# Stores of the pair matrices from another queue, other costs in the scheduler, and weight loads with a lead

## Chip, cores and metric

The kernel runs on one core of a Trainium2 chip. The time is that of one execution on the device, in microseconds. TensorE (PE) multiplies matrices, ScalarE (ACT) and VectorE (DVE) work on vectors, GpSimd (POOL) has little to do here, and SyncE (SP) issues transfers (DMAs).

## What is computed

Two layers of a network run over 1024 latent tokens and 256 context tokens of 1024 channels. One projection of the normalised input feeds four groups; group A is a gated DeltaNet over chunks of 64 tokens, in both directions, and it is the one that the change touches:

```python
decay = jnp.exp(jnp.where(incl, gcum[..., :, None] - gcum[..., None, :], -jnp.inf))
lmat = -jnp.where(strict, jnp.einsum('bnhid,bnhjd->bnhij', kb, kc) * decay, 0.0)
for _ in range(GDN_CHUNK_LOG2 - 1):      # tinv = (1 - lmat)^-1
    power = power @ power
    tinv = tinv + tinv @ power
attn = jnp.einsum('bnhid,bnhjd->bnhij', qc, kc) * decay
```

`lmat` and `attn` are the pair matrices, one of 64 x 64 for each chunk, head and direction. Groups B, C and D are convolutions and a gated MLP. All groups are gated by SiLU, joined, and go through one output projection, whose result is added to the input.

## The kernel before

In layer 0 the DeltaNet of the context stream (4 chunks) runs first and then that of the latent stream (16 chunks); so in layer 1. The dense projections of the other groups, 24 matmuls of 128 x 512 for a block (three for each of 8 slices of the weights, which are held as a high and a low part), are what PE does beside them.

A helper records every operation (so nearly all of them have line 215 in the profile), and a list scheduler, `schedule`, then puts them in one order for each engine. It goes by the costs of `estimate`, by a fixed price for a DMA, and by a priority: the place in the program plus a `boost`, a lower number going first. Where an operation can run on ACT or on DVE, it picks one. Each engine takes its instructions in that order. A DMA signals on one of eight semaphores, taken in turn in program order, and waits for the DMA eight before it, whichever queue that one is on.

The DeltaNet of a latent stream goes through these steps:

- `pair_matrices` runs eight times, for two chunks in each direction. It takes four of the six buffers `b` of 128 x 512: `gx` and `rw` are products made on DVE, PE sums `gx` up, ACT takes the exponential, DVE multiplies it in, PE multiplies keys and queries, and DVE masks the product and transposes it. Then it issues eleven stores on SP: two of `rw` into `at` (128 x 256, 128 KB each), and for each of three matrices into `zd` one of 128x2x64 (64 KB) and two of 64x2x64 (32 KB). The buffers come free when the stores have landed. Over both layers and streams these are 216 stores.
- `invert` runs twice (calls 1 to 4 of `pair_matrices` into the first half, 5 to 8 into the second). It loads blocks of 32 x 32 from `zd` into `u` (four loads), inverts them on DVE in 30 steps of two operations, and stores the result in `zb`.
- `scan` prepares each group of chunks: it loads from `zb`, transposes on DVE, and multiplies on PE (`ax<-b,b`, the first such matmul is where the preparation begins), and then goes through the chunks.

In the trace's names, in the latent stream of layer 0, the two halves of `zd` are `zd_550` and `zd_576`, the blocks are in `u_549`, the first inverse goes to `zb_580`, and `b_596` and `b_609` are temporaries of the two inversions.

Weights come in by `pump`: it loads them into one of two buffers `r` (512 KB), and `split` makes the high part on ACT (a cast, `w<-r`) and the low part on DVE. Only the split has a boost, of -600 (`AHEAD_SPLIT`).

Of the kernel before, what the change touches and what calls it, by code (L numbers as in the profile page):

```python
# [41 lines left out]
TC, G = 64, 4  # L42
# [37 lines left out]
class Program:  # L80
# [60 lines left out]
    def estimate(self, eng, method, out, ins, args, kw):  # L141
# [4 lines left out]
        if eng == "PE":  # L146
            if method == "transpose":
                return 0.12
            lhsT, rhs = ins[0], ins[1]
            n, m, k = self.cols(rhs), self.cols(lhsT), lhsT.shape[0]  # L150
            if "r" in str(rhs.dtype).split("float32")[-1]:
                return max(0.107, n / 2400.0 + 0.0133)
            if m <= 64 or k <= 64:
                return max(0.116, 0.01 + n * 4 / 2400.0) / (4 if self.quads else self.side_by_side(k, m))
            return max(0.214, n * 4 / 2400.0) if n > 16 else 0.4
        if eng == "ACT":
            return (0.051 if ps else 0.093) + n / 1200.0 + 0.093 * (ptr + acc)
        if eng == "DVE":
            if method == "reciprocal":
                return 0.07 + n * 0.00625  # L160
            if method in ("tensor_scalar", "tensor_copy") and not ps:
                return 0.069 + n / 1920.0 + 0.06 * ptr
            return 0.069 + n / 960.0 + 0.06 * ptr
# [23 lines left out]
    def add(self, calls):  # L187
# [16 lines left out]
        if eng == "SP":  # L204
            n = args[0].size() if callable(args[0].size) else args[0].size
            run = min(x.ap[-1][1] if x.ap[-1][0] == 1 else 1 for x in (args[0], args[1]))
            op.dma = n * 4 / 360e3 * (1.0 if run >= 128 else 2.0)
        for e, m, fn, ar, k in calls:
# [5 lines left out]
            cost = 0.475 if e == "SP" else self.estimate(e, m, o[0], n, ar, k)  # L214
# [43 lines left out]
    def schedule(self):  # L258
# [50 lines left out]
        while len(order) < len(ops):  # L309
# [68 lines left out]
            if e == "SP":  # L378
# [5 lines left out]
            for u in op.users:  # L384
                o = ops[u]
                o.ready_from.append((i, op.finish if e == "SP" else
# [80 lines left out]
class Block:  # L467
# [375 lines left out]
    def dense(self, items):  # L843
# [5 lines left out]
        def pump(i):  # L849
            while True:  # L850
# [13 lines left out]
                if q < min(i + 6, n) and self.room("r")() and (items[q].cond is None or items[q].cond()):  # L864
                    raws[q] = r = self.take("r", [P] + items[q].shape)
                    items[q].load(r)
                    st["l"] += 1
# [607 lines left out]
    def pair_matrices(self, st, c0, gi, s0, need_q):  # L1475
# [32 lines left out]
        if need_q:  # L1508
            nc.vector.tensor_tensor(rw, both(0), dm, ALU.mult)
            for d in range(2):  # L1510
                nc.sync.dma_start(st.at[d, :, c0:c0 + 2], rw[:, d].rearrange("p (c h) i -> p c (h i)", h=2))
        z = self.blk([P, 4, TC])
        nc.vector.transpose(z.rearrange("p a i -> p (a i)"), gx[:, 1].rearrange("p a i -> p (a i)"))
        for d, t in ((0, gx[:, 0]), (1, gx[:, 1]), (2, z)):
            to = zd[d, 2 * s0:2 * s0 + 4].rearrange("(c h) p i -> h p c i", h=2)
            t = t.rearrange("p (c h) i -> p h c i", h=2)
            nc.sync.dma_start(to[0], t[:, 0])
            for p in range(2):
                nc.sync.dma_start(to[1, (1 - p) * TC:(2 - p) * TC], t[p * TC:(p + 1) * TC, 1])
# [649 lines left out]
```

## Time and profile before

| what | value |
|---|---|
| median of 3 runs | 1415.69 us (1413.28 to 1418.06) |
| the profiled execution | 1418.21 us, of which the span 1416.1 |
| mean granted clock of PE | 0.943 |
| PE busy | 1277.3 us, 90% of the span |
| DVE busy | 986.6 us, 70% |
| ACT busy | 544.9 us, 38% |

Busy times are shares of the whole span. They say nothing of the stages, in which other engines wait or are waited for; the rows below are taken by stage. A row of the timeline has its start and its length, then engine, line and operation, `out<-in`, and how many instructions it joins; in brackets the idle time before it and what ended that. SPq is the time in which SP issues, no DMA's own duration.

### The profile page before, as it was taken

The page shows a single profiled execution, that of the slowest core. Times are in us where ns is not written, and L with a number is a line of the kernel's source. Part 1 is how long each engine was busy: PE and PEld are TensorE (multiplying, and loading weights), DVE is VectorE, ACT ScalarE, POOL GpSimd, SP SyncE. Part 2 cuts the span into 40 slices and gives each one's busy share as a digit, 9 for nine tenths or more (in the row PEclk, how much of TensorE's full clock was granted, in tenths as well). Part 3 has the DMA queues.
Part 4 walks back from the last instruction along what each step waited for, and adds up shares of the span by engine and source line. Part 5 has one row for each costly group of instructions (what it writes and reads, how often), then busy time and mean ns, then how long its engine had stood idle before and what let it go on. Part 6 is the DMA issues. An engine that isn't in the chain of part 4 may idle for free.

```text
span 1416.1 us, 27022 instructions
## 1 busy us (share of the span) xinstructions
PE 1277.3 (90%) x10888; PEld 1003.2 (71%) x10888; DVE 986.6 (70%) x2112; ACT 544.9 (38%) x917; POOL 11.9 (1%) x76
## 2 busy tenths in 40 slices
PE   6886699999988899999998999989998759999997
PEld 3875577986766655568886778978666646678886
DVE  4787969998855755573376669899776677784454
ACT  3876632254633122132154444343455303231221
POOL 1000000000000000000000000000000000000000
PEclk9997799999996889999999999999999779999999
DMA  9646332322447466573233332334226535132832
GB/s 310 182 108 183 108 89 62 88 46 58 104 105 172 121 178 193 179 223 104 90 112 109 114 104 63 67 81 101 62 50 147 136 85 127 51 105 89 262 84 56
DMA packets 310386, 166.75 MB, mean 118 GB/s; under 512 B 150174, under 2 KB 294902, under 8 KB 310262
## 3 DMA queue, kind: packets, MB, share of 16 engines
q1 hardware_dynamic: 310262, 165.03, 42.9%
q8 instruction: 85, 1.39, 0.4%
q14 instruction: 39, 0.32, 0.1%
HBM read 124.32 MB, written 35.42 MB: 113 GB/s over the span
## 4 chain that ended last, share of the span: by engine, by line
PE 52%; DVE 20%; DMA 12%; SPq 7%; ACT 5%; issue 4%; DVEq 0%; ACTq 0%; POOL 0%; POOLq 0%
PE mm L215 37%; DVE u L215 10%; PE sc L215 10%; SPq L215 7%; PE ax L215 5%; DVE b L215 5%; DMA x<-u 3%; DMA r<-in_w_in 3%; DVE w L215 2%; ACT b L215 1%; DMA u<-zd 1%; ACT L215 1%; DMA zd<-b 1%; ACT u L215 1%; DMA u<-in_x 1%
## 5 line engine op out<-in xcount | busy, mean ns | idle before, releaser
L215 PE MATMUL mm<-hh,w 128*128 128x512 f32 x1664 | 553.9, 407 | 6.8 <-ACT g L215 4.2
L215 PEld LDWEIGHTS mm<-hh,w 128*128 128x128 f32 x1664 | 316.1, 192 | 92.0 <-issue 20.8
L215 PE MATMUL mm<-hl,w 128*128 128x512 f32 x832 | 338.8, 407 | 1.5 <-issue 1.5
L215 PE MATMUL mm<-u,w 128*128 128x512 f32 (+1 forms) x1320 | 264.9, 359 | 13.9 <-ACT w L215 8.7
L215 PEld LDWEIGHTS mm<-u,w 128*128 128x128 f32 x1320 | 222.0, 195 | 48.1 <-ACT w L215 8.9
L215 DVE SCALAR_TENSOR_TENSOR u<-u,pv,u 128x1024 f32<-128x1024 f32 (+1 forms) x172 | 202.7, 1187 | 1.3 <-ACT u L215 0.6
L215 PEld LDWEIGHTS mm<-hl,w 128*128 128x128 f32 x832 | 159.9, 192 | 41.1 <-issue 9.4
L215 ACT CAST w<-r 128x1024 fp32r<-128x1024 f32 x88 | 92.5, 1052 | 249.5 <-PE mm L215 177.0
L215 DVE TENSOR_TENSOR w<-r,w 128x1024 fp32r<-128x1024 f32 x88 | 107.5, 1222 | 40.1 <-ACT w L215 39.8
L215 ACT ACT_TABLE_LOAD x87 | 111.6, 1283 | 21.4 <-DMA zd<-b 11.3
L215 DVE TENSOR_TENSOR u<-u,b 128x256 f32<-128x256 f32 (+26 forms) x246 | 90.1, 387 | 28.1 <-DMA u<-in_x 17.9
L215 ACT ACTIVATE b<-u 128x512 f32<-128x512 f32 (+1 forms) x71 | 42.5, 610 | 66.5 <-DVE u L215 45.5
L215 PE MATMUL mm<-u,u 128*128 128x256 f32 (+1 forms) x384 | 58.7, 303 | 5.7 <-ACT u L215 4.3
L215 DVE TENSOR_TENSOR b<-u 128x198 f32<-128x198 f32 (+24 forms) x180 | 56.9, 331 | 8.5 <-DMA u<-zd 6.9
L215 PEld LDWEIGHTS mm<-u,u 128*128 128x128 f32 x384 | 52.0, 201 | 9.0 <-ACT u L215 4.7
L215 PE MATMUL sc<-ident,b 128*128 128x128 f32 (+1 forms) x139 | 27.5, 322 | 25.2 <-ACT b L215 10.2
L215 PE MATMUL mm<-u,hh 128*128 128x272 f32 x256 | 48.5, 289 | 0.0
L215 PEld LDWEIGHTS sc<-v,u 64*64 64x64 f32 x1184 | 34.4, 140 | 19.6 <-DVE v L215 11.2
L215 PE MATMUL sc<-v,u 64*64 64x64 f32 x1184 | 42.9, 228 | 5.0 <-issue 4.0
L215 ACT COPY v<-sc 128x256 f32<-128x256 f32 x36 | 13.4, 372 | 78.6 <-PE sc L215 69.4
L215 ACT ACTIVATE b<-sc,mod,modG 128x128 f32<-128x128 f32 x86 | 35.0, 456 | 19.4 <-PE sc L215 11.0
L215 PEld LDWEIGHTS sc<-ident,b 128*128 128x128 f32 (+1 forms) x139 | 18.9, 163 | 32.6 <-ACT b L215 13.5
(273 smaller groups left out, 1455.6 us busy)
## 6 DMA issues: line engine op xcount, KB each, us to landing
r<-in_w_in SPq DMA_DIRECT2D x90, 512.0 KB
u<-in_w_ada SPq DMA_DIRECT2D x16, 1024.0 KB
u<-in_x SPq DMA_DIRECT2D x16, 512.0 KB
r<-ylat SPq DMA_DIRECT2D x16, 512.0 KB
ylat<-g SPq DMA_DIRECT2D x24, 256.0 KB
u<-in_w_out SPq DMA_DIRECT2D x12, 512.0 KB
at<-b SPq DMA_DIRECT2D x36, 128.0 KB
u<-at SPq DMA_DIRECT2D x18, 256.0 KB
```

Of the source, the lines that this page charges most:

```text
L215: op.alts[e] = ((lambda fn=fn, ar=ar, k=k: fn(*ar, **k)), cost, table)
```

## The change

The stores of `pair_matrices` are issued by `nc.scalar` in place of `nc.sync`, so that they stand in ACT's order. The costs in the scheduler are other numbers: a DMA's issue 0.62 in place of 0.475 us, on whichever engine, ACT's and DVE's fixed parts, small transposes on PE. The load of a weight in `pump` gets the same boost as its split.

```diff
             if method == "transpose":
-                return 0.12
+                return 0.11 if ins[0].shape[0] > 64 else 0.03
...
         if eng == "ACT":
-            return (0.051 if ps else 0.093) + n / 1200.0 + 0.093 * (ptr + acc)
+            return (0.155 if ps else 0.19) + n / 1200.0 + 0.05 * ptr + 0.093 * acc
         if eng == "DVE":
+            if n == 1:
+                return 0.155
...
+            if method == "tensor_tensor" and not ps and 128 < n <= 256:
+                return 0.4
...
-        if eng == "SP":
+        if method == "dma_start":
...
-            cost = 0.475 if e == "SP" else self.estimate(e, m, o[0], n, ar, k)
+            cost = 0.62 if method == "dma_start" else self.estimate(e, m, o[0], n, ar, k)
...
-            if e == "SP":
+            if op.dma:
                 dma_free = max(dma_free, t + 1.1) + op.dma
...
                     raws[q] = r = self.take("r", [P] + items[q].shape)
+                    self.nc.boost -= AHEAD_SPLIT
                     items[q].load(r)
+                    self.nc.boost += AHEAD_SPLIT
...
-                nc.sync.dma_start(st.at[d, :, c0:c0 + 2], rw[:, d].rearrange("p (c h) i -> p c (h i)", h=2))
+                nc.scalar.dma_start(st.at[d, :, c0:c0 + 2], rw[:, d].rearrange("p (c h) i -> p c (h i)", h=2))
...
-            nc.sync.dma_start(to[0], t[:, 0])
+            nc.scalar.dma_start(to[0], t[:, 0])
             for p in range(2):
-                nc.sync.dma_start(to[1, (1 - p) * TC:(2 - p) * TC], t[p * TC:(p + 1) * TC, 1])
+                nc.scalar.dma_start(to[1, (1 - p) * TC:(2 - p) * TC], t[p * TC:(p + 1) * TC, 1])
```

ACT in the latent stream of layer 0 before, from the exponential of the fifth call (`b_579`) to that of the sixth (`b_586`); `u_492` belongs to a convolution, `g_610` is a gate, `r` and `w` are weights:

```order
L215 ACTIVATE b_579<-ax_581 128x512
L215 ACT_TABLE_LOAD
L215 ACTIVATE u_492<-u_492 128x1024
L215 ACTIVATE g_610<-mm_608 128x512
L215 ACTIVATE g_610<-g_610,pv_71_166 128x512
L215 ACT_TABLE_LOAD
L215 ACTIVATE b_586<-sc_582 128x512
```

The same stretch of ACT now, from behind `b_579`, with the stores of the fifth call:

```order
L219 ACT_TABLE_LOAD
L219 ACTIVATE g_589<-mm_575 128x512
L219 ACTIVATE g_610<-mm_608 128x512
L219 DMA zd_576<-b_577 128x2x64
L219 DMA at_548<-b_578 128x256 x2
L219 DMA zd_576<-b_577 64x2x64 x2
L219 DMA zd_576<-b_577 128x2x64
L219 DMA zd_576<-b_577 64x2x64 x2
L219 DMA zd_576<-b_583 128x2x64
L219 DMA zd_576<-b_583 64x2x64 x2
L219 ACT_TABLE_LOAD
L219 ACTIVATE b_586<-sc_582 128x512
```

All eleven stores of a call now stand between its exponential and the next call's.

DVE in the same stream before, from the eighth call's mask and transpose (`b_599`, `b_603`) to the first steps of the first inversion (`b_596`); `x_637` and the rest belong to group D and the norms:

```order
L215 TENSOR_TENSOR b_599<-sc_602,b_601 128x512
L215 TENSOR_TENSOR b_600<-sc_602,b_601 128x512
L215 STREAM_TRANSPOSE b_603<-b_599 128x256
L215 TENSOR_TENSOR x_637<-sc_635,sg_411_508 128x256
L215 TENSOR_TENSOR x_637<-x_637,u_612 128x256
L215 TENSOR_SCALAR nq_517<-sc_617 128x16 x2
L215 TENSOR_TENSOR at_638<-sc_636,sg_411_508 128x256
L215 TENSOR_TENSOR b_596<-u_549 128x30
L215 TENSOR_TENSOR u_549<-u_549,b_596 128x30
L215 RECIPROCAL rn_421_518<-rn_421_518 128x32
L215 TENSOR_TENSOR b_596<-u_549 128x58
```

And now, around the same mask of the eighth call:

```order
L219 TENSOR_TENSOR u_549<-u_549,b_596 128x16x15
L219 TENSOR_TENSOR b_596<-u_549 128x240
L219 TENSOR_TENSOR u_549<-u_549,b_596 128x15x16
L219 TENSOR_TENSOR b_601<-b_601,b_600 128x512
L219 TENSOR_TENSOR b_596<-u_549 128x238
L219 TENSOR_TENSOR b_599<-sc_602,b_601 128x512
L219 TENSOR_TENSOR b_600<-sc_602,b_601 128x512
L219 STREAM_TRANSPOSE b_603<-b_599 128x256
L219 TENSOR_TENSOR w_658<-r_615,w_658 128x1024
L219 TENSOR_TENSOR x_637<-sc_635,sg_411_508 128x256
L219 TENSOR_TENSOR u_549<-u_549,b_596 128x14x17
L219 TENSOR_TENSOR x_637<-x_637,u_612 128x256
```

The eighth call's mask now stands between the two operations of the 17th of the first inversion's 30 steps, and the second inversion (`b_609`) begins when the first has ended, in place of running in turn with it.

SP ahead of the store of the first inverse, before:

```order
L215 DMA r_659<-in_w_in 128x8x128
L215 DMA gd_129<-g_657 64x512
L215 DMA r_702<-in_w_in 128x8x128
L215 DMA b_661<-in_smlp_w 128x4x128
L215 DMA zb_580<-u_549 128x1024
```

And now, with the block loads of the second inversion (`u_549<-zd_576`) ahead of it:

```order
L219 DMA gd_129<-g_645 64x512 x2
L219 DMA u_549<-zd_576 32x32x32 x3
L219 DMA b_628<-zd_550 32x8x32 x4
L219 DMA u_549<-zd_576 32x32x32
L219 DMA r_702<-in_w_in 128x8x128
L219 DMA gd_129<-g_657 64x512 x2
L219 DMA zb_580<-u_549 128x1024
```

The block loads wait for the stores of calls 5 to 8, and the store of the first inverse stands behind them.

On PE the first pair matmul of that stream moves from place 1881 to 1903 and the first matmul of the scan's preparation from 2386 to 2361. SP has 216 instructions less, ACT has 216 stores and 8 table loads more, and 52 operations move from ACT to DVE.

## Rows read from the trace of the kernel before

**Rows 1.** Windows: start:end, length; busy PE, PEld, DVE, ACT, POOL; PEclk; DMA; GB/s.
```profile
0.00:50.00 50.00, 34.33 (x262) 22.87 (x263) 24.46 (x100) 24.31 (x49) 3.75 (x36) 1.00 0.90 278
50.00:175.00 125.00, 89.94 (x683) 82.41 (x682) 105.35 (x296) 91.34 (x168) 1.34 (x6) 0.84 0.53 141
364.00:488.00 124.00, 108.27 (x699) 85.30 (x699) 86.98 (x203) 41.42 (x52) 0.31 (x2) 0.88 0.55 135
1044.00:1162.00 118.00, 91.36 (x597) 71.72 (x599) 86.52 (x193) 42.11 (x48) 1.47 (x7) 0.87 0.49 115
1275.00:1400.00 125.00, 125.00 (x553) 103.59 (x552) 60.33 (x112) 28.00 (x52) 0.00 (x0) 1.00 0.42 131
```

**Rows 2.** Timeline of PE: start, length; the scan's first preparation in either layer.
```profile
487.05 1.17 PE L215 MATMUL ax<-b,b 32*32 32x32 f32 x64 [3.25 <-DVE b L215]
1161.56 1.18 PE L215 MATMUL ax<-b,b 32*32 32x32 f32 x64 [12.20 <-DVE b L215]
```

**Rows 3.** Timeline of SP, first latent stream: first stores, last block loads, first inverse.
```profile
364.52 0.62 SPq L215 DMA_DIRECT2D zd<-b  x1
365.25 0.91 SPq L215 DMA_DIRECT2D at<-b  x2
...
421.82 5.11 SPq L215 DMA_DIRECT2D zd<-b  x8
...
436.31 2.03 SPq L215 DMA_DIRECT2D u<-zd  x3
...
475.42 0.46 SPq L215 DMA_DIRECT2D zb<-u  x1
```

**Rows 4.** Groups of ACT by form: count, busy us, mean ns, idle before them.
```profile
L215 ACT ACT_TABLE_LOAD x87 | 111.6, 1283 | 21.4 <-DMA zd<-b 11.3 <-DMA at<-b 3.5 <-DMA gd<-g 2.2
L215 ACT CAST w<-r 128x1024 fp32r<-128x1024 f32 x88 | 92.5, 1052 | 249.5 <-PE mm L215 177.0 <-DMA r<-ylat 31.8 <-DMA r<-in_w_in 31.8
L215 ACT ACTIVATE g<-mm 128x512 f32<-128x512 f32 x24 | 14.3, 594 | 21.3 <-PE mm L215 14.8 <-DMA ylat<-g 4.1 <-DMA gd<-g 2.4
L215 ACT ACTIVATE u<-u 128x1024 f32<-128x1024 f32 x12 | 12.7, 1060 | 13.5 <-DVE u L215 13.5
L215 ACT ACTIVATE b<-sc 128x512 f32<-128x512 f32 x15 | 9.0, 598 | 10.5 <-DMA zd<-b 10.4
L215 ACT ACTIVATE u<-u,pv 128x512 f32<-128x512 f32 x8 | 6.3, 814 | 6.9 <-DVE u L215 6.9
```

**Rows 5.** One call in the timeline (ACT, DVE) and one store's landing in the chain.
```profile
419.80 0.60 ACT L215 ACTIVATE b<-sc 128x512 f32<-128x512 f32 x1 [7.64 <-DMA zd<-b]
...
424.59 0.69 DVE L215 TENSOR_TENSOR b<-b,b 128x512 f32<-128x512 f32 x1
425.38 1.29 DVE L215 TENSOR_TENSOR b<-sc,b 128x512 f32<-128x512 f32 x2
...
420.19 2.00 DMA zd<-b
```

**Rows 6.** Timeline of SP, second layer: the first pair store and the first inverse.
```profile
1044.15 1.05 SPq L215 DMA_DIRECT2D zd<-b  x2
...
1152.04 0.40 SPq L215 DMA_DIRECT2D zb<-u  x1
```

**Rows 7.** Timeline of SP and PE in the context stage.
```profile
105.97 3.64 SPq L215 DMA_DIRECT2D zd<-b  x6
109.65 3.86 SPq L215 DMA_DIRECT2D u<-u  x6
...
114.19 1.06 SPq L215 DMA_DIRECT2D r<-in_w_in  x2
...
120.34 0.80 PE L215 MATMUL mm<-u,w 128*128 128x256 f32 x2 [8.65 <-ACT w L215]
122.36 0.80 PE L215 MATMUL mm<-u,u 128*128 128x256 f32 x2 [1.23 <-ACT u L215]
...
133.99 0.63 PE L215 MATMUL sc<-ones,b 64*64 64x1 f32 x16 [2.43 <-ACT b L215]
```

**Rows 8.** Timeline of SP at the start: the last adaLN load.
```profile
27.54 1.06 SPq L215 DMA_DIRECT2D whl<-in_w_ada  x1
```

**Rows 9.** Waits of the DMA queue: us in total, times, longest.
```profile
SPq L215 <- DMA r<-in_w_in: 30.6, 15, 4.1
```

More of the change, by code (lines that the diff above doesn't have):

```diff
@@ L385, in schedule @@
                 o = ops[u]
-                o.ready_from.append((i, op.finish if e == "SP" else
+                o.ready_from.append((i, op.finish if op.dma else
                                      {x: op.finish + (0.12 if x == "SP" else self.LAT[e, x]) for x in o.alts}))
```

## The prediction, made before the change was run

> **What bounds the kernel now.** I read the stretches first, then in each of them who waits for whom. TensorE (PE) has no gap in the output projections: 553 matmuls fill 125.00 us of 125.00 [rows 1], so nothing is to be gained there but less work. The time that can go is PE's idle time beside the gated DeltaNet: 35 us in 50 to 175 (context stream), 15.7 in 364 to 488 (first latent stream), 26.6 in 1044 to 1162 (second) [rows 1]. In the last two the stretch ends when the scan's first preparation on PE starts, at 487.05 and 1161.56, and there PE waits for VectorE, which waits for the inverted matrices [rows 2].
>
> What these wait for stands in the queue of SyncE (SP). Its first store of a pair matrix of the first latent stream goes out at 364.52 and the last block loads of it at 436.31 [rows 3]: 71.8 us, in which it issues 88 stores. Eight `zd` stores in a row take 5.11 us, 0.64 each, two `at` stores 0.91, 0.455 each [rows 3]. 72 x 0.64 + 16 x 0.455 = 53.4 us, so three quarters of the stretch is issuing. ScalarE (ACT) stands behind it: an exponential waited 7.64 us for a buffer that a store had to give back [rows 5]. Then come the inversion on VectorE (DVE) and its store, issued at 475.42 [rows 3]. The same in the second layer goes from 1044.15 to 1152.04 [rows 6]. So the queue of SP is what bounds these two stages, and ACT has room in them: 41.4 us of 124.0 and 42.1 of 118.0 busy [rows 1].
>
> **The change part by part.** *The stores on ACT.* The trace has no DMA that ACT issues, so the price of one is bounded: from below, nothing but the dispatch (ACT's compute goes on beside it), from above SP's 0.64 and 0.455 on ACT's own time. I take SP's, since those are the only rows of an issue, and they are of the same transfers. The order of the changed kernel puts between the first and the last store of the first latent stream 88 stores, 15 table loads, 8 exponentials or roots, 6 SiLU out of PSUM, 5 casts of weights, 4 SiLU with a parameter and one of 1024 columns on ACT, that is 39 instructions beside the stores. With the durations of [rows 4]: 53.4 + 15 x 1.283 + 8 x 0.598 + 6 x 0.594 + 5 x 1.052 + 4 x 0.814 + 1.060 = 53.4 + 19.2 + 17.9 = 90.5 us, 11.3 per call of `pair_matrices`. The way through one call gives nearly the same: table load and exponential 1.9, then DVE's product and the first of the two with the mask, 424.59 to some 426.7, 2.1 [rows 5], then eleven stores 6.7, that is 10.7, as a call's exponential stands behind the stores of the call before. In the second layer 88 stores, 14 table loads and 15.7 us of the rest make 87.1, 10.9 per call.
>
> So the calls don't become shorter: SP had 9 us for one, ACT will have 11. What becomes shorter is what comes behind them. Before, the block loads for the first inversion stood among the stores of the later calls and the inversion ran after all eight. Now they stand right behind the fourth call's stores, and the order of DVE puts the inversion beside calls 5 to 8, its steps from the 17th on behind the eighth call's mask. Those 14 steps and what stands among them are some 10 us, so it ends at about 7 x 11.3 + 10 = 89 us. But the store of its result stands on SP behind the block loads of the second inversion (three, then a fourth, with four `b` loads between) and three more transfers, and these loads wait for the last store of call 8 to land. So the store goes out at 90.5 + 2.0 (landing, [rows 5]) + 11 issues x 0.64 = 99.5 us after the first store. Before it was 475.42 - 364.52 = 110.9 [rows 3]. **Gain 11.4 in layer 0.** The way from that store to PE is as long as before (11.6 us, 475.42 to 487.05 [rows 2, 3]).
>
> In layer 1: 87.1 + 2.0 + 12 issues x 0.64 = 96.8, against 1152.04 - 1044.15 = 107.9 [rows 6]. **Gain 11.1.**
>
> *What the new order does on PE.* The list scheduler, with its new costs, puts the first pair matmul of the first latent stream behind 22 more dense matmuls, 5.0 us at 125.00 / 553 = 0.226 each [rows 1], and the scan's preparation ahead of 25, 5.7 us, that stood before it. The stage begins 5.0 later, and 5.7 of work is left to be done after it: 11.4 - 5.0 - 5.7 = 0.7 us gained in layer 0. In layer 1 it begins 28 matmuls, 6.3 us, later and the same matmuls stand ahead of the preparation: 11.1 - 6.3 = 4.8 gained.
>
> *Weight loads ahead, and SP without the stores.* In the context stage PE waited 8.65, 1.23 and 2.43 us in a row behind weight casts and what follows them [rows 7]; the two loads that they needed went out at 114.19, behind six `zd` stores of 3.64 us, six `u` and others [rows 7]. Without the stores, and with the loads ahead, I expect those 12.3 us to shrink. Against that stand 22 stores, 13 us, on an ACT that was busy 91.3 of 125 us there with DVE at 105.4 of 125 [rows 1]. From a gain of 12 to a loss of 13: I take a gain of 5, since ACT's sum, 104 of 125, still fits.
>
> *The start.* Four weight loads are issued earlier than before; two of them, 1 MB in all, now stand ahead of the last adaLN load, which went out at 27.54 [rows 8]. At the 278 GB/s of the first 50 us [rows 1] that is 3.8 us for it; what PE does with the weights earlier gives some back. Loss 2 (0 to 4).
>
> *PSUM.* SiLU evacuations on ACT now can stand behind a batch of stores of 6.7 us. Two further buffers of 24 matmuls at 0.226, 10.8 us, cover that; where they don't, PE stands. Loss 2 (0 to 20, were half of the 24 SiLU [rows 4] late by 1.7). Eight more table loads and 52 small operations moved from ACT to DVE lie in the sums above or beside PE's full stretches, where DVE is busy 60.3 of 125 us [rows 1]: 0.
>
> **Sum**: -0.7 - 4.8 - 5 + 2 + 2 = -6.5. The profiled run took 1418.2 us, the median of the runs is 1415.7; 1411.7 by the one, 1409.2 by the other, and I say 1410.
>
> **Against the Trainium skill.** SP's rows show 0.64 us of issue per store, and these add up to three quarters of the stage. The Trainium skill (DMA: Bandwidth & Descriptors, Issuing engines are not separate DMA queues) says that queues of several engines run on the same DMA engines, so that issuing elsewhere saves the issue time alone. By that the stage would lose nothing but this, and ACT pays it back: that is the rival "idle only moves" below. And the Trainium skill (Perfetto Trace Analysis, DVE / Act Engine Instruction) has an engine's sequencer hand compute to a queue and go on to the next instruction; no row here shows ACT do so around a DMA. By it ACT's stores would run beside its SiLU and casts: the rival "stores beside compute".
>
> **The rivals.** *Stores beside compute (faster).* If an issue doesn't hold ACT's compute, a call takes its own chain, 10.7 less what the next call's table load hides, 9.4 us: 8 x 1.9 + 8 x 1.5 = 27 us less, of which the DVE, with some 87 us busy in either stage [rows 1], lets about half through, and ctx gains 10 in place of 5. 1410 - 14 - 5 = 1391 us. For it: SP's rows time an issue and no work of a vector unit. Against it: the stores wait for DVE's products of the same call.
>
> *ACT becomes the bound (slower).* Each store on ACT stands in line with the compute. A DMA also waits for the transfer eight before it in program order, on either queue, and in the new order 77 ACT stores wait so for a transfer of SP, 14 of them a load of weights. SP's own waits for those cost 30.6 us in 15 times [rows 9], 2.0 each. 14 x 2.0 = 28 us, nearly all in the stages that bound: 1410 + 28 = 1438 us. It decides from 0.4 us more per call on (16 calls, 6.5 us to lose). For it: ACT at 11.3 per call has no slack. Against it: without its 53 us of stores SP has most of those 72 us free, so that a transfer eight back can be issued and land in time.
>
> *Idle only moves (same).* DVE, busy 87 of 124 us [rows 1], sets the calls whoever issues, and the start gives back what ctx brings: 1412 to 1420 us, 1416. The same time would come if the compiled order did not do what its plan says, with stores waiting in ACT for the tiles of DVE.
>
> **How the numbers follow.** Forecast 0.40, around 1410 (half of it below 1411); stores beside compute 0.22; ACT as bound 0.26; idle only moves 0.12. The range from 1388 to 1434 takes in the faster rival nearly whole and the lesser half of the slower one. A measurement of this kernel tells about 0.3%, 4.2 us, from no change. Faster by more than that: 0.22, half of the forecast's 0.40, and 0.03 of idle-only-moves, 0.45. Within it: 0.14 of the forecast and 0.09 of idle-only-moves, 0.23. Slower: 0.26 and 0.06 of the forecast, 0.32.
>
> **What would show it.** In the profile after: stores on ACT's queue at 0.6 us with ACT's compute standing still behind them (the forecast) or running through them (the faster rival); ten to eleven us from exponential to exponential; the store of the first inversion 99.5 us after the first pair store, not 111; the first steps of the inversion ahead of the last pair stores; PE without the 8.65 us gap in the context stage. I am wrong if the calls take over 12 us each, which idle time of ACT behind transfers of SP would show, or if PE shows new gaps behind SiLU evacuations.

## The result, and the profile after

The changed kernel takes 1423.91 us in the median of 20 runs (1412.89 to 1429.43), the kernel before 1415.45 in 20 runs beside it (1408.3 to 1422.97): a ratio of 1.0052, with a 95% interval of 1.0033 to 1.0071. It is 8.5 us slower, where 6 us faster was forecast. The profiled execution is by chance the fastest of the 20, 1412.89 us, while that of before lay 2.8 above its median. The two spans (1411.2 and 1416.1) therefore show the wrong sign, and I read idle time of PE in their place, since the matmuls are the same 10888: span less PE's busy time is 1416.1 - 1277.3 = 138.8 us before and 1411.2 - 1262.9 = 148.3 after. So PE idles 9.5 us more in these two executions, near the 8.5 us between the medians. Against it stands the granted clock, 0.943 and 0.946 in the two profiles; in the median of the changed kernel's runs it is 0.938.

The windows after; columns as in [rows 1], ahead of PEclk the busy times of PE, PEld, DVE, ACT and POOL:

```profile
0.00:50.00 50.00, 29.83 (x226) 19.86 (x227) 24.71 (x85) 22.14 (x39) 3.84 (x36) 0.93 0.94 284
50.00:175.00 125.00, 90.70 (x688) 82.88 (x687) 109.57 (x322) 85.88 (x157) 1.34 (x6) 0.84 0.50 133
364.00:488.00 124.00, 105.78 (x791) 81.81 (x791) 88.76 (x187) 49.95 (x61) 0.32 (x2) 0.89 0.54 133
488.00:625.00 137.00, 121.61 (x2119) 74.54 (x2114) 81.11 (x206) 30.65 (x63) 0.20 (x4) 0.94 0.59 177
1044.00:1162.00 118.00, 88.53 (x676) 69.16 (x674) 86.88 (x186) 40.28 (x50) 1.47 (x7) 0.83 0.47 114
```

Before, the window from 488 had 7.1 us of idle time:

```profile
488.00:625.00 137.00, 129.89 (x2222) 78.20 (x2210) 77.50 (x178) 34.68 (x74) 0.20 (x4) 0.91 0.63 185
```

So PE's idle time is 4.5 us longer at the start, 0.8 shorter in the context stage, 2.5 longer in the first latent stage, 8.3 longer behind it, and 2.8 longer in the second. These come to 17.3 us; the other stretches give back 7.8 (2.8 in 175 to 364, 3.5 in 625 to 1044, 1.6 behind 1162, by rounded figures). Four places in the traces tell why.

**The start.** SP's timeline after:

```profile
0.80 2.10 SPq L219 DMA_DIRECT2D r<-in_w_in  x4
2.95 0.44 SPq L219 DMA_DIRECT2D b<-in_c  x1
```

PE's timeline after, the first matmul of all:

```profile
7.68 0.26 PE L219 MATMUL sc<-ident,b 16*128 16x16 f32 x1 [7.68 <-DMA b<-in_c_ctx]
```

The same matmul before:

```profile
3.01 0.26 PE L215 MATMUL sc<-ident,b 16*128 16x16 f32 x1 [3.01 <-DMA b<-in_c_ctx]
```

Four weight transfers stand ahead of the two small loads of `c` (`in_c`, `in_c_ctx`), for which the first matmul waits, and it starts 4.7 us later.

**A call on ACT.** ACT's own queue (ACTq) and its compute: the first store, the fifth to seventh call, the last stores:

```profile
367.76 0.38 ACTq L219 DMA_DIRECT2D zd<-b  x1
...
419.48 6.32 ACTq L219 DMA_DIRECT2D zd<-b  x8
425.89 1.28 ACT L219 ACT_TABLE_LOAD   x1 [7.11 <-DMA zd<-b]
427.18 0.60 ACT L219 ACTIVATE b<-sc 128x512 f32<-128x512 f32 x1
427.80 1.28 ACT L219 ACT_TABLE_LOAD   x1
429.09 0.60 ACT L219 ACTIVATE g<-mm 128x512 f32<-128x512 f32 x1
429.33 0.38 ACTq L219 DMA_DIRECT2D zd<-b  x1
429.58 0.59 ACT L219 ACTIVATE g<-mm 128x512 f32<-128x512 f32 x1
429.93 0.83 ACTq L219 DMA_DIRECT2D at<-b  x2
430.79 5.54 ACTq L219 DMA_DIRECT2D zd<-b  x8
436.36 1.28 ACT L219 ACT_TABLE_LOAD   x1 [6.18 <-DVE b L219]
...
453.51 7.77 ACTq L219 DMA_DIRECT2D zd<-b  x9
```

An issue costs ACT nearly what it cost SP: eight `zd` stores take 5.54 us, 0.69 each (0.64 in [rows 3]). The compute ahead of a store still runs while it is issued (429.33 lies inside the row from 429.09), the compute behind the stores waits for the last of them (436.33, then 436.36). From the first to the last store it is 93.5 us (367.76 to 461.28), where [rows 3] has 71.8. From exponential to exponential it is 10.5 to 14.6 us, 12.0 in the mean; the prediction had ten to eleven, and over 12 as a sign that it was wrong. In the longest of these, DVE waited 5.13 us for a transfer of SP (`u<-u`).

**The two inverses.** SP, after: the last blocks for the second inversion, the store of the first inverse, that of the second:

```profile
460.66 3.86 SPq L219 DMA_DIRECT2D u<-zd  x3
...
466.75 0.58 SPq L219 DMA_DIRECT2D u<-zd  x1
...
469.99 0.54 SPq L219 DMA_DIRECT2D zb<-u  x1
...
513.72 0.33 SPq L219 DMA_DIRECT2D zb<-u  x1
```

The first comes 102.2 us after the first store, where it was 110.9 [rows 3]. The second comes 146.0 after it, where it was 121.2: 485.67 - 364.52, by these rows of SP before, the last block load and that store:

```profile
447.21 0.63 SPq L215 DMA_DIRECT2D u<-zd  x1
...
485.67 0.34 SPq L215 DMA_DIRECT2D zb<-u  x1
```

So the last blocks for the second inversion, which went out 82.7 us after the first store (447.21, behind the loads at 436.31 that the prediction took for the last), go out 99.0 us after it now. The first inversion itself ends on DVE 101.2 us after the first store, at 468.91, having waited 3.06 us on the way for a cast that ACT made behind its stores. DVE after:

```profile
463.96 1.23 DVE L219 TENSOR_TENSOR w<-r,w 128x1024 fp32r<-128x1024 f32 x1 [3.06 <-ACT w L219]
...
468.72 0.19 DVE L219 TENSOR_TENSOR u<-u,b 128x30 f32<-128x30 f32 x1
```

**What PE does with that.** PE after: a wait in the pair stage, the first preparation, and the second:

```profile
407.96 1.97 PE L219 MATMUL sc<-u 64*64 64x128 f32 x16 [8.33 <-DVE b L219]
...
481.34 0.75 PE L219 MATMUL ax<-b,b 32*32 32x32 f32 x64
...
524.60 1.18 PE L219 MATMUL ax<-b,b 32*32 32x32 f32 x64 [10.59 <-DVE b L219]
```

The second preparation before, without a wait:

```profile
511.21 0.59 PE L215 MATMUL ax<-b,b 32*32 32x32 f32 x44
```

The first preparation no longer waits at all, as forecast (3.25 us in [rows 2]), and starts 5.7 us earlier. The second, of which the prediction does not speak, waits 10.59 us for the second inverse and starts 13.4 us later. Before, both inversions ran in turn on DVE ahead of the scan. Now the blocks of the second arrive only when the first is done, and DVE's order has put its steps among the scan's operations (`x`, `at`, `v`), which wait in turn for PE or ACT:

```profile
503.72 0.42 DVE L219 TENSOR_TENSOR x<-x,u 128x256 f32<-128x256 f32 x1
504.05 0.42 DVE L219 TENSOR_TENSOR at<-sc,sg 128x256 f32<-128x256 f32 x1
504.39 0.34 DVE L219 TENSOR_TENSOR u<-u,b 128x184 f32<-128x184 f32 x1
504.76 0.33 DVE L219 TENSOR_TENSOR b<-u 128x168 f32<-128x168 f32 x1
505.80 0.43 DVE L219 TENSOR_TENSOR v<-sc,sg 128x256 f32<-128x256 f32 x1 [0.71 <-ACT v L219]
```

### The profile page after: what moved, and what is told of

It is laid out like the page before. It is cut to its first block, busy times and chain, and to the rows that moved or that the text cites. A ratio compares the mean times of both kernels' runs of the same rounds, so it can differ in the third digit from the quotient of the medians.

```text
span 1411.2 us, 27024 instructions
## 1 busy us (share of the span) xinstructions
PE 1262.9 (89%) x10888; PEld 994.4 (70%) x10888; DVE 1007.0 (71%) x2164; ACT 530.0 (38%) x873; POOL 12.0 (1%) x76
## 4 chain that ended last, share of the span: by engine, by line
PE 59%; DMA 14%; DVE 13%; ACT 5%; issue 4%; ACTq 2%; SPq 2%; DVEq 0%
PE mm L219 45%; PE sc L219 9%; DMA x<-u 6%; DVE u L219 6%; PE ax L219 5%; DVE b L219 4%; DMA r<-in_w_in 3%; ACTq L219 2%; ACT b L219 2%; DMA zd<-b 2%; SPq L219 2%; DVE w L219 1%; ACT u L219 1%; ACT L219 1%; DMA whl<-in_w_ada 1%
## 5 line engine op out<-in xcount | busy, mean ns | idle before, releaser
L219 PE MATMUL mm<-hh,w 128*128 128x512 f32 x1664 | 547.7, 402 | 3.2 <-DVE w L219 1.4
L219 PEld LDWEIGHTS mm<-hh,w 128*128 128x128 f32 x1664 | 312.1, 189 | 86.6 <-issue 18.2
L219 PE MATMUL mm<-hl,w 128*128 128x512 f32 x832 | 334.8, 402 | 0.0
L219 PE MATMUL mm<-u,w 128*128 128x512 f32 (+1 forms) x1320 | 261.5, 355 | 2.9 <-ACT u L219 1.7
L219 PEld LDWEIGHTS mm<-u,w 128*128 128x128 f32 x1320 | 218.2, 190 | 37.1 <-ACT u L219 2.1
L219 DVE TENSOR_TENSOR b<-u 128x108 f32<-128x108 f32 (+20 forms) x180 | 58.3, 325 | 4.9 <-DMA u<-zd 2.1
L219 PE MATMUL sc<-ident,b 128*128 128x128 f32 (+1 forms) x139 | 28.0, 336 | 31.3 <-DVE b L219 14.6
L219 PEld LDWEIGHTS mm<-u,hh 128*128 128x128 f32 x256 | 41.4, 194 | 3.7 <-DVE u L219 3.7
L219 DVE TENSOR_TENSOR u<-u,mm 128x512 f32<-128x512 f32 (+1 forms) x30 | 18.9, 630 | 31.3 <-PE mm L219 31.3
```

The costliest lines, as they stand in the source:

```text
L219: op.alts[e] = ((lambda fn=fn, ar=ar, k=k: fn(*ar, **k)), cost, table)
```

## The experiments

The theory on reading this (A): the lead costs at the start; the stores on ACT make the pair stage 20 us longer, so that the second inverse comes late; the costs do nothing. Rivals: B, the stores on ACT gain and the lead loses it; C, only the clock differs. Later ones stand where they come up. All times are medians, with the ratio to the kernel before, run beside them, and its 95% interval. Beside each kernel the one before had a median of its own, 1414.45 to 1417.16 us, and a ratio is taken from all runs, so that it can differ by some 0.1% from the quotient of two medians. "Way" is from the first to the last pair store, layer 0 and layer 1; "inverses" is from the first pair store to the store of the first and second inverse, layer 0.

| kernel | time | ratio (95%) | way | inverses |
|---|---|---|---|---|
| before | 1415.45 | 1 | 71.8, 79.2 | 110.9, 121.2 |
| changed | 1423.91 | 1.0052 (1.0033 to 1.0071) | 93.5, 91.5 | 102.2, 146.0 |
| e1 stores back on SP | 1429.54 | 1.0099 (1.0073 to 1.0125) | 70.8, 68.3 | 119.9, 122.5 |
| e2 no lead | 1420.40 | 1.0038 (1.0014 to 1.0062) | 93.8, 93.4 | 105.6, 150.4 |
| e3 ACT alone | 1430.09 | 1.0105 (1.0083 to 1.0128) | 98.7, 94.3 | 111.1, 152.8 |
| e4 costs alone | 1434.65 | 1.0129 (1.0106 to 1.0151) | 67.4, 66.9 | 120.3, 122.8 |
| e5 lead later | 1423.32 | 1.0057 (1.0036 to 1.0077) | 94.8, 92.0 | 105.7, 150.2 |
| e6 split | 1389.07 | 0.9829 (0.9809 to 0.9850) | 83.7, 71.2 | 107.4, 129.0 |
| e7 short inversion | 1420.83 | 1.0048 (1.0027 to 1.0069) | 92.6, 91.7 | 102.2, 147.7 |
| e8 either queue | 1407.04 | 0.9946 (0.9926 to 0.9966) | 81.1, 70.4 | 105.8, 131.1 |
| e9 inverse first | 1428.84 | 1.0089 (1.0069 to 1.0108) | 94.0, 93.2 | 102.0, 148.5 |
| e10 split, inverse first | 1401.02 | 0.9886 (0.9865 to 0.9908) | 85.8, 77.8 | 108.8, 132.4 |
| e11 split, old costs | 1401.38 | 0.9894 (0.9874 to 0.9914) | 88.4, 77.7 | 106.1, 135.6 |
| e12 inverse close | 1436.84 | 1.0135 (1.0111 to 1.0159) | 93.2, 93.7 | 102.8, 132.6 |
| e13 split, inverse close | 1394.90 | 0.9829 (0.9802 to 0.9857) | 84.3, 71.8 | 108.3, 128.8 |
| e14 no table loads | 1416.08 | 0.9998 (0.9979 to 1.0018) | 90.4, 90.3 | 99.5, 144.5 |
| e15 seven buffers | 1414.49 | 0.9996 (0.9979 to 1.0014) | 85.0, 88.8 | 93.9, 141.9 |
| e16 split, seven buffers | 1391.30 | 0.9833 (0.9804 to 0.9863) | 71.5, 64.4 | 102.4, 121.5 |
| e17 only `at` on ACT | 1413.60 | 0.9993 (0.9975 to 1.0011) | 67.2, 62.4 | 113.3, 120.4 |

### One part at a time: e1 to e4

e1 undoes the first part, in all three store lines:

```diff
-                nc.scalar.dma_start(st.at[d, :, c0:c0 + 2], rw[:, d].rearrange("p (c h) i -> p c (h i)", h=2))
+                nc.sync.dma_start(st.at[d, :, c0:c0 + 2], rw[:, d].rearrange("p (c h) i -> p c (h i)", h=2))
```

> The changed kernel with its stores on SP again, costs and weight lead kept. Theory A (the lead costs at the start, the stores on ACT cost at the second inverse): the 4.5 us that PE loses in the first 50 us stay, the second inverse is stored some 10 us behind the first again (44 in the changed kernel), so about 4 us better than the changed kernel and 4 slower than before, 1419 us. Theory B (the stores on ACT gain and only the lead loses): slower than the changed kernel, 1428 us or more. Theory C (the granted clock makes the difference and idle time does not): the time of the changed kernel, 1424 us, at a clock near 0.938.

e2 undoes the lead:

```diff
-                    self.nc.boost -= AHEAD_SPLIT
                     items[q].load(r)
-                    self.nc.boost += AHEAD_SPLIT
```

> The changed kernel without the boost of the weight loads: stores on ACT and new costs alone. Theory A: the first load of c is issued first again, PE's first matmul at about 3 us in place of 7.7, the first 50 us lose 15.7 us of idle time as before; the second inverse still late: 1424 - 4.5 = 1419 us. Theory B: faster than the kernel before, about 1410 us. Theory C: 1424 us.

e3 makes the first part alone, on the kernel before (`nc.scalar` in the three lines, a DMA at 0.475 on either engine):

> The kernel before with its pair stores on ACT and nothing else (a DMA still costs 0.475 us in the plan). Theory A: first inverse some 9 us earlier, second inverse some 25 us later than before, 3 to 5 us slower than before, 1419 us. Theory B: faster than before, about 1409 us. Theory C: as before within 0.3%, 1415 us, unless the clock is lower.

e4 makes the second part alone, the new costs:

> The kernel before with the new costs in the scheduler alone; stores on SP, no lead. Theory A: within 0.3% of before, 1415 us, since the stores on SP still set the stage. Theory B: the same. Theory C: the same.

None of the theories stands as it was. The costs alone, which move no store, lose 18.5 us; on top of them the stores on ACT gain 14 (1434.65 to 1420.40), while on the old costs they lose 14. So neither part has a price of its own: each draws a new order of all engines, and orders differ by as much as the whole question. Theory C falls: e3 and e4, which it had at 1415 us, take 1430.09 and 1434.65, and e4 has 165.2 us of PE idle time (1429.3 less 1264.1 busy) against 138.8. What holds of A is local, and the same in the kernels so far with all stores on ACT (changed, e2, e3): a way of 91 to 99 us and a second inverse at 138 or later in both layers, where the stores on SP give 67 to 79 and 119 to 123. In layer 0 PE waits 10.3 to 12.2 us for DVE at the second preparation in all of them (changed, e2, e3, and e5, e7, e9 below), 9.2 in e14, and in none with the stores on SP (before, e1, e4); e15 below is the exception. In layer 1 a second inverse as late costs no such wait: 0.10 us in the changed kernel. e3's row:

```profile
528.44 1.18 PE L215 MATMUL ax<-b,b 32*32 32x32 f32 x64 [12.16 <-DVE b L215]
```

Of the lead: e2 has the start back and loses the context stage, 13.9 and 40.8 us of idle time where the changed kernel has 20.2 and 34.3:

```profile
0.00:50.00 50.00, 36.09 (x276) 24.56 (x277) 26.15 (x100) 22.92 (x43) 3.75 (x36) 1.00 0.91 278
50.00:175.00 125.00, 84.22 (x646) 76.21 (x645) 109.32 (x310) 84.61 (x152) 1.34 (x6) 0.82 0.51 136
```

So the gain that the forecast saw in the context stage is there, 6.5 us, and the start takes it back with 6.3.

### Lead later, stores split: e5, e6, e8

e5 leaves the first four weight loads where they were:

```diff
-                    self.nc.boost -= AHEAD_SPLIT
+                    self.loads = getattr(self, "loads", 0) + 1
+                    lead = AHEAD_SPLIT if self.loads > 4 else 0
+                    self.nc.boost -= lead
...
```

> The changed kernel with the weight lead from the fifth load on, so that the loads of c go first at the start again. Theory A (the lead loses at the start because the load of c stands behind two weights, and gains in the context stage): PE's first matmul at 3 us in place of 7.7, idle time of the first 50 us near 15 in place of 20.2, idle time of 50 to 175 near 34 as in the changed kernel: 5 us better than it, 1419 us. Theory B (the gain in the context stage came with the weights that were early at the start): idle of 50 to 175 back at 41, the time of the kernel without lead, 1420 us.

Both halves of A came true in idle time, 13.5 us in the first 50 and 35.1 in 50 to 175, and its time did not: it is the changed kernel's, 1423. Over the whole span PE idles 145.2 us against 148.3, so that 3.1 of the 6.7 us gained at the start are left, too little for these intervals to tell. In the profiled execution the granted clock of 50 to 175 is also lower, 0.77 where it was 0.84, and PE did 650 matmuls there, not 688:

```profile
50.00:175.00 125.00, 89.87 (x650) 82.12 (x649) 110.16 (x310) 87.36 (x156) 1.35 (x6) 0.77 0.50 136
```

e6 divides the stores of a call; e8 lets the scheduler choose the queue of each (`nc.either` with SP and ACT for the three lines):

```diff
-            nc.scalar.dma_start(to[0], t[:, 0])
+            (nc.scalar if d == 1 else nc.sync).dma_start(to[0], t[:, 0])
             for p in range(2):
-                nc.scalar.dma_start(to[1, (1 - p) * TC:(2 - p) * TC], t[p * TC:(p + 1) * TC, 1])
+                (nc.scalar if d == 1 else nc.sync).dma_start(to[1, (1 - p) * TC:(2 - p) * TC], t[p * TC:(p + 1) * TC, 1])
```

> As e5, and of the eleven stores of a call six (two zd matrices) go back to SP and five (the two at, one zd matrix) stay on ACT. Theory A (eleven stores on one queue make a call 11.7 us on ACT, which brings the blocks of the second inversion late): a call takes 9 us or less, the second inverse is stored 20 us earlier than the 513.7 of the changed kernel, PE loses 8 us less in 490 to 650: 1410 us. Theory B (the calls are set by DVE and PE, whoever issues): calls of 11 us as before, time as e5, 1419 us.

> As e5, and the scheduler may put each pair store on SP or ACT, whichever is free earlier in its plan; it puts about half on either. Theory A: as e6, calls of 9 us or less and 1410 us. Theory B: as e5, 1419 us; or worse, if stores of one call that wait for each other's landing hold both queues.

e6 is the best kernel of all, 24 to 26 us faster than before and 21 below what theory A had. The queues issue side by side, here ACT's in the third call:

```profile
388.78 0.45 ACTq L219 DMA_DIRECT2D zd<-b  x1
389.62 0.91 ACTq L219 DMA_DIRECT2D at<-b  x2
390.56 1.32 ACTq L219 DMA_DIRECT2D zd<-b  x2
```

And SP's in the same call:

```profile
388.77 3.56 SPq L219 DMA_DIRECT2D zd<-b  x6
```

A batch takes 3.6 us where it took 6 to 7, and a call 10.5 us in layer 0, where theory A had 9 or less, and 8.9 in layer 1. The second inverse is 129.0 us behind the first store, PE has no wait at the second preparation, and in layer 1 the inverses come at 95.0 and 110.7 where before had 107.9 and 121.4, though PE waits 19.70 us at the first preparation there. PE idles 1386.8 - 1265.4 = 121.4 us against 145.2 in e5, with 16.0 of the difference in 364 to 625, and the clock is 0.946 (median of the runs) against 0.938. e8 has nearly the same way, and the same inverses in layer 0, and is 18 us slower; in layer 1 its first inverse comes at 102.3, 7.3 us behind that of e6, and what its order loses elsewhere is open.

### The second inversion: e7, e9, e12, e10, e13

e7 keeps the order of every engine and lets each of the second inversion's operations work on one column, by another call behind the recorded one:

```diff
+            if n == 16 and gi == 1:
+                ra, rb = nc.vector.real, X3[:, 0:1, p + 1:p + 2]
+                fns = (lambda t=tmp[:, 0:1, 0:1], a=X3[:, 0:1, p:p + 1], b=X3[:, p:p + 1, p + 1:p + 2]: ra.tensor_tensor(t, a, b, ALU.mult),
+                       lambda t=tmp[:, 0:1, 0:1], b=rb: ra.tensor_tensor(b, b, t, ALU.add))
...
```

> The changed kernel with every engine's order kept, where the 30 steps of the second inversion of both latent streams work on one column in place of up to 240 (that inversion is left out of the computation). Theory A (the second inverse is what PE waits for at 524.6, 10.6 us): it is stored some 13 us earlier, the wait of 10.6 us ends, idle of 490 to 650 falls from 15.9 to about 7, 8 us in layer 0 and up to 5 in layer 1: 1411 to 1416 us. Theory B (the wait would go to another tile of the same preparation): idle of 490 to 650 stays above 13, 1421 us or more.

The operations are short, by this row of DVE late in the inversion:

```profile
513.74 0.16 DVE L1554 TENSOR_TENSOR b<-u 128x1 f32<-128x1 f32 x1
```

The inverse isn't earlier for it, 147.7, and PE waits as long:

```profile
531.98 1.18 PE L219 MATMUL ax<-b,b 32*32 32x32 f32 x64 [10.56 <-DVE b L219]
```

Theory A fails with that; idle of 490 to 650 is 15.5 us, on B's side, though the wait is at the same tile. So it is not the length of the inversion's operations on DVE that makes it late. Its steps stand in line behind the scan's. That gave theory A2 (the weaving is the cause) and D (the idle time would only move).

e9 raises `AHEAD_INV` from 0 to 1000:

> The changed kernel with a boost of 1000 in place of 0 for both inversions, above the scan's 800, so that DVE takes the steps of the second inversion ahead of the scan's operations in place of between them. Theory A2 (the second inverse is late because its steps stand among the scan's, each of which waits for PE): the second inverse is stored within 25 us of the first, against 44 in the changed kernel; PE's wait of 10 us at the second preparation gets under 5; 5 to 8 us less in layer 0 and some in layer 1: 1413 us. Theory D (the late second inverse is only where idle time shows that the 92 us of stores bring in any case, so it moves to another wait): 1420 us or more.

It tells nothing of either: the steps depend on each other, and the scheduler went on filling the gaps between them with the scan's, so the second inverse is still 46.5 us behind the first (44 in the changed kernel). e12 therefore moves them by hand, behind the planned order:

```diff
+        for k, mine in self.close.items():
+            at = order.index(self.step0[k])
+            late = [i for i in mine if order.index(i) > at]
+            inside = set(late)
+            order = order[:at] + late + [i for i in order[at:] if i not in inside]
...
```

`mine` are the second inversion's operations and its store, `step0` the scan's first operation on `v`.

> The changed kernel with every order kept but one: of the second inversion, the steps that DVE had between the scan's operations now stand together ahead of the first of these, and the store of its result behind them. Theory A2 (PE's wait of 10.6 us at the second preparation comes of this weaving): the second inverse is stored at about 496 in place of 513.7, the wait at the second preparation gets under 4 us, idle of 490 to 650 falls by 5 to 8: 1417 us. Theory D (the scan loses on DVE what the second preparation gains): idle of 490 to 650 stays within 2 us of 15.9, 1424 us.

A2 fails, and it is worse than D had it: idle of 490 to 650 is 21.1 us. The inverse is 13.4 us earlier, and PE waits for the scan first and for the preparation still, 11.07 and 6.31 us; the time is 13 us longer, with 160.9 us of idle time in both layers together against 148.3:

```profile
505.58 1.12 PE L220 MATMUL sc<-v,u 64*64 64x64 f32 x16 [11.07 <-DVE v L220]
...
541.00 1.17 PE L220 MATMUL ax<-b,b 32*32 32x32 f32 x64 [6.31 <-DVE b L220]
```

When the second blocks arrive only at the scan's start, some 20 us of DVE (60 operations, 0.33 in the mean in the changed kernel) must go ahead of the scan or among it, and PE waits either way. That leaves their arrival as the cause; no run moved it with the rest of the order held.

e10 and e13 make the moves of e9 and e12 on e6:

> The split of e6 with the same boost of the inversions. Theory A2: the second inverse is 21.6 us behind the first in layer 0 of e6; that shrinks by 5 to 10, and the time from 1389 to some 1384 us. Theory D: no change to e6 within 0.3%, 1389 us.

> The split of e6 with the same move. Theory A2: e6 has no wait at the second preparation, so nothing is to be gained: 1389 us within 0.3%. Theory D: the scan's delay costs, 1393 to 1400 us.

There is nothing to gain there: e13 is the same as e6 within the intervals (0.9829 both), and e10, whose boost changes the whole order, is 8 us slower by the ratios, with the second inverse no nearer to the first (23.6 us behind it).

### What makes a call as long as it is: e14 to e17, e11

e14 keeps every order and puts a SiLU behind the recorded exponential:

```diff
+        op = nc.ops[-1]
+        op.alts["ACT"] = (lambda o=dm, x=pe, f=nc.scalar.real: f.activation(o, x, AF.Silu),) + op.alts["ACT"][1:]
```

> The changed kernel with every order kept, where the exponential of the pair matrices is a SiLU (another function, so the decay is left out of the computation), which takes 28 table loads of 1.28 us away from ACT. Theory A (a call is as long as ACT's stores and compute add up to): the way from first to last store falls from 93.5 to 76 to 80 us, PE's waits behind the pair matmuls (8.3 us at 408) shrink, both inverses come 13 us or more earlier: 1400 to 1408 us. Theory F (the calls are set by DVE, PE and the landing of stores, and the table loads stand in idle time): 90 us or more from first to last store, 1420 us or more.

The time is 8 us better, that of before, but the way is only 3 us shorter in layer 0 and 1 in layer 1, with 28 table loads gone, so F is nearer, though its time, 1420 or more, didn't come either. ACT now has gaps of up to 5.5 us between its compute and the next stores, and what a call waits for is seen on DVE: `rw`, the product with `wn`, waits for a buffer that the stores of the call before give back, and in one call DVE stands behind a transfer of SP that comes late. e14's DVE:

```profile
411.03 0.69 DVE L219 TENSOR_TENSOR u<-u,nk 128x512 f32<-128x512 f32 x1 [5.63 <-DMA u<-u]
...
422.40 0.69 DVE L219 TENSOR_TENSOR b<-wn,RX 128x512 f32<-128x512 f32 x1 [4.41 <-DMA zd<-b]
...
431.08 0.69 DVE L219 TENSOR_TENSOR b<-wn,RX 128x512 f32<-128x512 f32 x1 [4.07 <-DMA zd<-b]
```

The same waits stand in the changed kernel (5.28 us in the sixth call; 5.35 in the fifth, which the profile puts down to a block load), there with ACT's table loads inside them. So theory G, that buffers bind. e15 is `"b": 7` in `CAPS`, e16 the same on e6, and e17 is e6 with only `at` on ACT:

> The changed kernel with seven buffers b in place of six. Theory G (a call waits for buffers that the stores of the call before give back, 4 to 5 us of DVE in each): the way from first to last store falls from 93.5 to 85 us or less, and the time by 5 us or more, to 1418 or less. Theory A (ACT's own sum): 93 us and 1424 us, give or take 6 that another order brings.

> The split of e6 with seven buffers b. Theory G: the way from first to last store falls from 83.7 to under 76 us in layer 0, and the time by up to 8 us, 1381 to 1389. Theory A: as e6 give or take 6.

> As e6, with only the two at stores of a call on ACT and the nine zd stores on SP. If two queues side by side are what the split brings, nine on SP make 5.8 us of a call against 3.9 and 3.0 in e6: first to last store 5 us longer, between e1 (1429) and e6 (1389), some 1400 us. If the split's gain is mostly that at no longer holds the queue: 1389 us.

G holds for the stage: the way falls by 8.5 us in layer 0 and 2.7 in layer 1. The time is that of before, some 8 us less than the changed kernel's by the ratios; since the whole order changed with the seventh buffer, it isn't shown that the shorter way brings this. The second inverse is nearly as late as in the changed kernel (141.9 us), and yet PE waits only 0.05 us at the second preparation: its order now has more dense matmuls ahead of that, and the idle time stands in the pair stage, 25.8 us where the changed kernel has 18.2. So where PE idles depends on its order as well as on the inverse. e15's windows:

```profile
364.00:488.00 124.00, 98.20 (x758) 72.83 (x757) 87.14 (x185) 46.56 (x59) 0.31 (x2) 0.83 0.52 125
488.00:625.00 137.00, 135.41 (x2174) 86.50 (x2172) 85.13 (x209) 32.34 (x66) 0.20 (x4) 1.00 0.63 187
```

On the split the way falls by 12 and 7 us, too, and the time not at all: there the way no longer binds. For e17 neither expectation came true: it has the shortest way of all, not 5 us more, and 24 us more time than e6. Its first inverse is late again (113.3 and, in layer 1, 106.4): with nine `zd` stores and all block loads on SP, the first block load goes out at 432.68, behind the last store, where e6 has it at 408.20, among the stores. What sets e6 apart is both inverses early, not the shortest way.

e11 is e3 with the division of e6:

> The kernel before with five of a call's eleven stores on ACT and nothing else: old costs in the plan, no lead. Theory A (both queues issue side by side, and that shortens the way from the first store to both inverses): the first inverse 100 us or less after the first store in layer 1 and the second within 115, as in e6; faster than before by about 20 us, 1395 us. Theory E (the gain of e6 came with the new costs and the later lead, which fit the split): within 0.5% of before, 1410 to 1418 us.

A holds in the main, 15 us faster than before without new costs or lead; the inverse is at 96.5 and 118.7 in layer 1, near what was expected. The 9 to 12 us from there to e6 belong to costs and lead together, which were not taken apart here.

## Why the prediction was wrong, step by step

**The price of a store and the length of a call** were nearly right: 0.69 measured against 0.64, 93.5 us for eight calls against 90.5, and 91.5 against 87.1 in layer 1. The reason given was only half of it. The step took ACT's rows for a sum, and e14 shows that the sum is not the bound: without 28 table loads the way is 3 us shorter. A call also waits for buffers that the stores of the call before give back; with one buffer more (e15) the way is 8.5 us shorter. So that the sum came out within 3 us is in part luck.

**The first inverse** came at 102.2 us (99.5 forecast, [rows 3] 110.9), and the first preparation without a wait. That is luck in part, too: the prediction let the inversion end at 89 us and its store wait for SP's transfers, while the inversion ended at 101.2, about 1 us ahead of these. In layer 1 the inverse came at 103.1 (96.8 forecast), so that 4.8 us were gained and not 11.1; the term missed 4.4 us of the longer way and 1.9 behind it. There SP had its transfers out at 1144.5 and stood waiting for DVE until the store at 1146.65, by its waits in 1144 to 1147:

```profile
SPq L219 <- DVE b L219: 2.3, 1, 2.3
```

**The step that failed** is "the stage begins 5.0 later, and 5.7 of work is left to be done": it ends layer 0 at the first preparation. The second inversion was mentioned there only as what stands ahead of a store, and not asked when it would itself be done. Counted from the first store it was done 25 us later than before; PE waited 10.59 us for it and idled 8.3 us more behind the stage: forecast 0.7 gained in layer 0, measured 2.5 + 8.3 lost in idle time. e7 and e12 show that it can't be had back by shorter operations or another place for them; e6 and e16, where the inverse comes earlier, don't have the wait. e15 doesn't either, with the inverse at 141.9, but idles in the pair stage in its place; how much of the loss the late inverse makes by itself is open.

**The start** was costed by the last adaLN load. The first load of all, `c`, stood behind the same weights, and PE's idle time grew by 4.5 us, not 2. **The context stage** gained 0.8, not 5: the lead did bring 6.5 us there (e2), and ACT's stores with the new order took 5.7. **PSUM** evacuations cost nothing that the trace shows: PE's waits at `mm` for ACT's `g` are 0.4 us in all, 4.2 before.

**The costs** were taken as free except for the order that they drew around the pair stage. That order is not the same price by price: e4 loses 18.5 us with them alone.

**The rivals.** "ACT becomes the bound" had the sign, at 1438; its mechanism, stores that wait for a transfer of SP eight before, I did not find as a cause: in the changed kernel's pair stage ACT's compute waits mostly behind its own stores, and no run took the waits for SP away. Its sign, ACT idle behind a transfer of SP, is there in one call of layer 0, by way of DVE (5.13 us). "Stores beside compute" has one part in the trace: compute ahead of a store runs on beside its issue. "Idle only moves" describes it best, with a place that it didn't name.

**The Trainium skill.** By the Trainium skill (DMA: Bandwidth & Descriptors, Issuing engines are not separate DMA queues), issuing DMAs on several engines saves only the time of the issue. With all stores moved the runs agree, and nothing was saved, since ACT pays 0.69 us for each. With the stores divided, two sequencers issue one call's stores at once, and a batch takes 3.6 us in place of 6 to 7. e6 is 1.7% faster; since e17 uses both queues, too, and is no faster than before, the issue time saved does not explain the gain by itself. By the Trainium skill (Perfetto Trace Analysis, DVE / Act Engine Instruction), the sequencer hands compute to a queue and goes on. The trace agrees as far as 429.33 lies inside the row from 429.09: a store's issue does not wait for compute ahead of it. Compute behind a store waits, by 436.36.

Open is how much of any time here belongs to the mechanism and how much to the new order it draws. The orders were held in e7 and e14, nearly in e12, and in e13 against e6; in all other kernels the whole order changed, and pairs of before, changed and e1 to e4 that differ in one part differ by -14 to +19 us.

## What to carry to other kernels

Here moving a queue's work onto an engine that also computes made the serial part longer (93.5 us against 71.8), and dividing it over both took part of that back (83.7). A shorter serial part is not yet a faster kernel: e17 has the shortest, 67.2, and the time of before. Follow each product of the stage to its last reader, not to the first that waits today: here the first inverse came 9 us earlier and the second 25 us later, and PE waited for the second. And where a scheduler draws the order, a change of its costs is a change of everything; measure it by itself before adding another.

## What the runs showed of the hardware

A store costs ACT 0.38 to 0.7 us of issue in the changed kernel, near SP's 0.455 to 0.64 before [rows 3]; ACT's compute goes on under the issue of a store that stands behind it (429.33), and in all eight calls of layer 0 the next compute starts within 0.1 us of the last issue's end.

The granted clock of 50 to 175 was 0.84 in the changed kernel's profile and 0.77 in that of e5, both means between its levels of 1.2 GHz (0.5) and 2.4 GHz (1). That the earlier start of e5 brought the lower clock isn't shown: e14 starts as late as the changed kernel, with 20.2 us of idle time in the first 50, and has 0.78, while e2 and e4, with 13.9 and 13.7, have 0.82 and 0.81. Why it differs stays open. e14's window:

```profile
50.00:175.00 125.00, 94.00 (x671) 86.58 (x670) 106.45 (x315) 81.85 (x155) 1.10 (x2) 0.78 0.49 129
```
